# Reciprocal square roots in a two-layer hybrid encoder: a GpSimd power and one Newton step instead of a bit trick and three Newton steps

## The chip, the cores and the metric

The kernel runs on one core of a Trainium2 chip. The metric is the device time of one execution in microseconds (us). The core's engines each work through a queue of their own, in the order in which the program was built: PE (TensorE, matrix products; PEld is its weight load), DVE (VectorE), ACT (ScalarE), POOL (GpSimd) and SP (SyncE, which issues the loads). They wait for one another by semaphores. An instruction whose wait is not over holds up everything behind it on the same engine.

## The reference: two layers of FFN, mixer, FFN

The input x is 256 tokens of width 1024, float32. Each of two layers adds a gated feed-forward network, a mixer and a second feed-forward network, each behind a normalisation of its input. After the second layer comes a last normalisation.

```python
def rms_norm(x, g):
    xf = x.astype(jnp.float32)
    y = xf * lax.rsqrt(jnp.mean(xf * xf, axis=-1, keepdims=True) + EPS)
    return (y * g.astype(jnp.float32)).astype(x.dtype)

def l2_norm(x):
    xf = x.astype(jnp.float32)
    return xf * lax.rsqrt(jnp.sum(xf * xf, axis=-1, keepdims=True) + EPS)

for l in range(DEPTH):
    x = x + 0.5 * swiglu(rms_norm(x, ln_ffn1[l]), ffn1_w_in[l], ffn1_w_out[l])
    x = x + hybrid_mixer(rms_norm(x, ln_mix[l]), ...)
    x = x + 0.5 * swiglu(rms_norm(x, ln_ffn2[l]), ffn2_w_in[l], ffn2_w_out[l])
return rms_norm(x, ln_final)
```

The mixer has three branches: a windowed attention (6 heads), a differential attention (4 heads, with rms_norm over each head's output) and a gated delta rule in both directions (6 heads: a short convolution over q, k and v, silu, l2_norm of q and k, a triangular solve and a scan over chunks of 64 tokens, and rms_norm over each head's output times silu of a gate). Their outputs go through one output projection.

## The kernel before: stages, queues and the places that take a reciprocal root

x stays on chip, channels on the 128 partitions, as 8 blocks of 128 x 256. The weights stream in by 512 KB loads that SP issues; up to 8 are in flight or waiting (`wr`).

In an FFN each product of float32 matrices is made of three products of split halves (L259 to L261). ACT rounds each weight block to its high half `wh` (L253), DVE subtracts to get the low half `wl` (L254), PE multiplies. The norm is folded out: PE works on the unnormalised x, and the factor of each token is multiplied into the results (`rb`, L277). So PE starts an FFN before the norm is known, and the norm's small products stand a few blocks later in PE's queue.

In a mixer, `ORDER` is a list of pieces; it is the order in which the pieces are written down. The tile framework's scheduler then builds each engine's queue from the pieces, by its own estimates of when an operand will be ready, so neighbouring pieces interleave. PE's products there write banks of three small pools of PSUM. `pm`, with two banks, serves among others the projections (`pj`), the attention scores (`pss`) and the output projection (`py`): a third product can't begin until the first one's bank has been read out by DVE or ACT.

The pieces that matter here, in order of the program, with the names of the trace:

- `norm_scale` (L193 to L216), for each norm over the width: PE sums the squares of each token (`f_ps`, `m_ps`, `fin_ps`; L200), DVE scales them (`f_v`, L204), `rsqrt` gives the roots of 128 x 2 values (`f_r`, `m_r`, `fin_r`), and PE spreads them over the partitions (`f_pb`, L209). It is called for the four FFNs (f), the two mixers (m) and the end (fin).
- `qk_norm` (`qn` in `ORDER`, L580 to L593), twice in a mixer: ACT squares (`sqt`), DVE sums to `ss` (L586, L587), `rsqrt` on 128 x 12 values, and DVE multiplies q or k by the result (`raw`, L593). After it PE transposes q and k (`pkq`) and multiplies them (`pq`), and DVE inverts the triangular blocks, row by row (`L`, `Vi`, `pp`; L799 and L800). Between them in DVE's queue stand convolution taps (`pad`, L550), read-outs of projections (`pad<-pj`, L537) and gated outputs (`cs`, L571).
- `diff_norm` (`dn`, L763 to L774), once in a mixer: `rsqrt` on 128 x 8 values.
- `out_norm` (`on`, L1004 to L1013), twice in a mixer, one for each half of the tokens: `rsqrt` on 128 x 6 values (`m0on`), beside the first part of the output projection, whose results DVE adds to x (`x<-x,py`, L1031).

That makes 17 calls of `rsqrt` in both layers: 7 on 128 x 2 (4 f, 2 m, 1 fin), 4 on 128 x 12, 2 on 128 x 8 and 4 on 128 x 6.

Before the change `rsqrt` is 11 instructions on DVE: a shift and an integer subtraction that give a first guess (L167, L169), and three Newton steps of three instructions each (L172, L173, L175). In each of them an operand is the result of the one before.

POOL has little to do: 135 instructions, 82.9 us of the span. Its first arithmetic instruction (`sqacc`, L191) has a row "ISA" ahead of it in its queue, which reloads the engine's library of functions.

Of the kernel before, what the change touches and what calls it, by code (L numbers as in the profile page):

```python
# [7 lines left out]
F32 = mybir.dt.float32  # L8
F32R = mybir.dt.float32r
BF16 = mybir.dt.bfloat16  # L10
I32 = mybir.dt.int32
AF = mybir.ActivationFunctionType
ALU = mybir.AluOpType
# [3 lines left out]
P = 128  # L17
# [40 lines left out]
class Kernel:  # L58
    def __init__(self, ctx, tc, ins, out):
        self.tc, self.nc, self.ins, self.out = tc, tc.nc, ins, out  # L60
        nc = self.nc
        ec = ctx.enter_context
        self.cp = ec(tc.tile_pool(name="cp", bufs=1))
        self.wp = ec(tc.tile_pool(name="wp", bufs=4))
        self.rp = ec(tc.tile_pool(name="rp", bufs=NRAW))
        self.xp = ec(tc.tile_pool(name="xp", bufs=1))
        self.sp = ec(tc.tile_pool(name="sp", bufs=2))
        self.pools = {
            t: ec(tc.tile_pool(name=t, bufs=n, space=PSUM)) for t, n in (("pm", 2), ("pd", 4), ("pt", 2))
        }  # L70
        cp = self.cp
        self.x = self.xp.tile([P, KD, S], F32, tag="x", name="x")
        self.col = cp.tile([P, 150], F32, name="col")
        self.cst = None
        self.onec = cp.tile([P, 1], F32, name="onec")
        nc.vector.memset(self.onec, 1.0)
        warm = cp.tile([P, 1], F32, name="warm")
        nc.scalar.activation(warm, self.onec, AF.Copy)

# [83 lines left out]
    def rsqrt(self, v, n, name, out=None):  # L163

        nc, sp = self.nc, self.sp
        ti = sp.tile([P, n], I32, tag=f"rs_i{n}", name=f"{name}_i")
        nc.vector.tensor_scalar(ti, v.bitcast(I32), 1, None, ALU.arith_shift_right)  # L167
        y = sp.tile([P, n], F32, tag=f"rs_y{n}", name=f"{name}_y")
        nc.vector.tensor_scalar(y.bitcast(I32), ti, -1.0, float(0x5F3759DF), ALU.mult, ALU.add)  # L169
        a = sp.tile([P, n], F32, tag=f"rs_a{n}", name=f"{name}_a")  # L170
        for i in range(3):
            nc.vector.scalar_tensor_tensor(a, v, -0.5, y, ALU.mult, ALU.mult)  # L172
            nc.vector.tensor_tensor(a, a, y, ALU.mult)  # L173
            o = y if i < 2 or out is None else out
            nc.vector.scalar_tensor_tensor(o, a, 1.5, y, ALU.add, ALU.mult)  # L175
        return o

    def sq_add(self, k, eng=None, last=False):
# [1057 lines left out]
```

## Time and profile before

| | |
|---|---|
| time, median of 3 runs | 1163.51 us (1162.44 to 1164.4) |
| the profiled execution: time, span | 1162.4 us, 1160.6 us |
| PE busy | 1122.9 us (97%) |
| DVE busy | 735.1 us (63%), 1442 instructions |
| ACT busy | 523.0 us (45%) |
| POOL busy | 82.9 us (7%) |
| mean granted TensorE clock | 0.978 |

The span runs from the first to the last instruction; 1.8 us of the time lie outside it. The busy time of PE is modelled with overlaps, so 97% says that PE seldom stood still, not that it ran at its peak. Layer 0 has its first FFN from 0 to 199 us, its mixer to about 383 us and its second FFN to about 590 us; layer 1 follows 569 us later, stage by stage, and the last norm begins at 1148 us. POOL is the engine with most room, DVE the one on which the removed instructions stand.

### The profile page before, as it was taken

The page shows a single profiled execution, that of the slowest core. Times are in us where ns is not written, and L with a number is a line of the kernel's source. Part 1 is how long each engine was busy: PE and PEld are TensorE (multiplying, and loading weights), DVE is VectorE, ACT ScalarE, POOL GpSimd, SP SyncE. Part 2 cuts the span into 40 slices and gives each one's busy share as a digit, 9 for nine tenths or more (in the row PEclk, how much of TensorE's full clock was granted, in tenths as well). Part 3 has the DMA queues.
Part 4 walks back from the last instruction along what each step waited for, and adds up shares of the span by engine and source line. Part 5 has one row for each costly group of instructions (what it writes and reads, how often), then busy time and mean ns, then how long its engine had stood idle before and what let it go on. Part 6 is the DMA issues. An engine that isn't in the chain of part 4 may idle for free. (4 is left out here: it accounts for less than half of the span.)

```text
span 1160.6 us, 21957 instructions
## 1 busy us (share of the span) xinstructions
PE 1122.9 (97%) x8970; PEld 1025.6 (88%) x8970; DVE 735.1 (63%) x1442; ACT 523.0 (45%) x967; POOL 82.9 (7%) x135
## 2 busy tenths in 40 slices
PE   7999999998899999999999999999989999999996
PEld 7999999776668999999999999988756789999996
DVE  7666654678746566665566666547886476666643
ACT  6545432263572454544444454414437435445431
POOL 0000002101202100000000000011020020000010
PEclk9999999997899999999999999999978999999998
DMA  9655643521114555565555565534210254556521
GB/s 335 213 184 182 206 165 102 163 79 51 54 56 132 189 174 184 184 204 170 173 173 182 182 201 181 160 117 127 78 51 37 75 193 153 184 183 201 182 89 37
DMA packets 49637, 173.64 MB, mean 150 GB/s; under 512 B 5504, under 2 KB 6784, under 8 KB 49536
## 3 DMA queue, kind: packets, MB, share of 16 engines
q1 hardware_dynamic: 49104, 171.64, 45.1%
q8 instruction: 70, 1.15, 0.4%
q10 hardware_dynamic: 432, 0.60, 0.1%
q14 instruction: 31, 0.25, 0.1%
HBM read 171.17 MB, written 1.05 MB: 148 GB/s over the span
## 5 line engine op out<-in xcount | busy, mean ns | idle before, releaser
L254 DVE TENSOR_TENSOR wl<-wr,wh 128x1024 fp32r<-128x1024 f32 x254 | 310.9, 1225 | 181.9 <-ACT wh L253 181.8
L253 ACT ACTIVATE wh<-wr 128x1024 fp32r<-128x1024 f32 x254 | 267.3, 1053 | 256.2 <-issue 146.4
L261 PE MATMUL ps<-xh,wl 128*128 128x256 f32 x1336 | 378.3, 283 | 0.8 <-DVE wl L254 0.8
L259 PE MATMUL ps<-xh,wh 128*128 128x256 f32 x1336 | 379.0, 284 | 0.1
L260 PE MATMUL ps<-xl,wh 128*128 128x256 f32 x1336 | 378.0, 283 | 0.0
L261 PEld LDWEIGHTS ps<-xh,wl 128*128 128x128 f32 x1336 | 256.4, 192 | 1.2 <-DVE wl L254 1.2
L259 PEld LDWEIGHTS ps<-xh,wh 128*128 128x128 f32 x1336 | 256.4, 192 | 1.0 <-issue 0.6
L260 PEld LDWEIGHTS ps<-xl,wh 128*128 128x128 f32 x1336 | 256.4, 192 | 0.0
L259 PE MATMUL ps<-hh,wh 128*128 128x256 f32 x672 | 190.5, 284 | 0.0
L261 PE MATMUL ps<-hh,wl 128*128 128x256 f32 x672 | 188.0, 280 | 0.0
L260 PE MATMUL ps<-hl,wh 128*128 128x256 f32 x672 | 187.5, 279 | 0.0
L428 PE MATMUL pj<-xf,wr 128*128 128x256 f32 x544 | 132.6, 399 | 2.9 <-issue 2.6
L259 PEld LDWEIGHTS ps<-hh,wh 128*128 128x128 f32 x672 | 125.7, 187 | 3.6
L260 PEld LDWEIGHTS ps<-hl,wh 128*128 128x128 f32 x672 | 126.3, 188 | 0.0
L261 PEld LDWEIGHTS ps<-hh,wl 128*128 128x128 f32 x672 | 126.2, 188 | 0.0
L428 PEld LDWEIGHTS pj<-xf,wr 128*128 128x128 f32 x544 | 106.9, 202 | 19.7 <-issue 3.3
L191 POOL TENSOR_TENSOR sqacc<-sqacc,sqt 128x256 f32<-128x256 f32 x41 | 34.6, 843 | 742.0 <-ACT sqt L187 741.9
L282 ACT ACTIVATE hh<-h 128x256 fp32r<-128x256 f32 x88 | 36.1, 415 | 90.3 <-DVE h L280 90.3
L277 DVE TENSOR_TENSOR t<-ps,f_rb 128x256 f32<-128x256 f32 x88 | 36.9, 424 | 37.7 <-PE ps L261 37.4
L1024 PE MATMUL py<-oT,wr 128*128 128x256 f32 x256 | 59.1, 384 | 0.0
L283 DVE TENSOR_TENSOR hl<-h,hh 128x256 fp32r<-128x256 f32 x88 | 36.8, 423 | 30.4 <-ACT hh L282 30.4
L1024 PEld LDWEIGHTS py<-oT,wr 128*128 128x128 f32 x256 | 47.2, 190 | 7.3 <-DVE x L1031 0.3
(321 smaller groups left out, 1135.7 us busy)
## 6 DMA issues: line engine op xcount, KB each, us to landing
wr<-in_ffn SPq DMA_DIRECT2D x258, 512.0 KB, 3.4
wr<-in_mix SPq DMA_DIRECT2D x50, 512.0 KB, 3.4
wr<-in_mix SPq DMA_DIRECT2D x8, 408.0 KB, 3.1
wr<-in_mix SPq DMA_DIRECT2D x8, 384.0 KB, 3.0
x<-in_x SPq DMA_DIRECT2D x4, 256.0 KB, 4.3
ar<-in_ffn SPq DMA_DIRECT2D x8, 128.0 KB, 3.9
cb<-in_constb SPq DMA_DIRECT2D x1, 588.0 KB, 9.8
out_y<-fo SPq DMA_DIRECT2D x2, 256.0 KB, 2.4
```

Of the source, the lines that this page charges most:

```text
L191: (eng or nc.gpsimd).tensor_tensor(self.sq, self.sq, t, ALU.add)
L253: nc.scalar.activation(h, w, AF.Copy)
L254: nc.vector.tensor_tensor(lo, w, h.bitcast(F32), ALU.subtract)
L259: mm(out, lhsT=ah, rhs=bh, start=start, stop=False)
L260: mm(out, lhsT=ah, rhs=bl, start=False, stop=False)
L261: mm(out, lhsT=al, rhs=bh, start=False, stop=stop)
L277: nc.vector.tensor_tensor(t[:rows], gate, rb[:rows], ALU.mult)
L282: nc.scalar.activation(hh[:n, j, :], h[:n], AF.Copy)
L283: nc.vector.tensor_tensor(hl[:n, j, :], h[:n], hh[:n, j, :].bitcast(F32), ALU.subtract)
L428: mm(ps[:, 0:S], lhsT=w[:, k * P : (k + 1) * P], rhs=xf[:, k, :], start=k == 0, stop=k == KD - 1)
L1024: mm(ps[:, 0:S], lhsT=st["o", q // NBLK][:, c], rhs=oT[:, k, :], start=k == ks[0], stop=k == ks[-1])
```

## The change: what it does

`rsqrt` asks POOL for v to the power of -0.5 (`tensor_tensor` with `pow`, the exponent read from a tile `mhalf` of 128 x 12 that is filled once) and takes one Newton step on DVE, three instructions, where there were eleven. Each call now goes from DVE to POOL and back.

```diff
@@ -74,6 +74,8 @@
         self.onec = cp.tile([P, 1], F32, name="onec")
         nc.vector.memset(self.onec, 1.0)
+        self.mhalf = cp.tile([P, 12], F32, name="mhalf")
+        nc.vector.memset(self.mhalf, -0.5)
@@ -163,16 +165,13 @@
     def rsqrt(self, v, n, name, out=None):
         nc, sp = self.nc, self.sp
-        ti = sp.tile([P, n], I32, tag=f"rs_i{n}", name=f"{name}_i")
-        nc.vector.tensor_scalar(ti, v.bitcast(I32), 1, None, ALU.arith_shift_right)
         y = sp.tile([P, n], F32, tag=f"rs_y{n}", name=f"{name}_y")
-        nc.vector.tensor_scalar(y.bitcast(I32), ti, -1.0, float(0x5F3759DF), ALU.mult, ALU.add)
+        nc.gpsimd.tensor_tensor(y, v, self.mhalf[:, 0:n], ALU.pow)
         a = sp.tile([P, n], F32, tag=f"rs_a{n}", name=f"{name}_a")
-        for i in range(3):
-            nc.vector.scalar_tensor_tensor(a, v, -0.5, y, ALU.mult, ALU.mult)
-            nc.vector.tensor_tensor(a, a, y, ALU.mult)
-            o = y if i < 2 or out is None else out
-            nc.vector.scalar_tensor_tensor(o, a, 1.5, y, ALU.add, ALU.mult)
+        nc.vector.scalar_tensor_tensor(a, v, -0.5, y, ALU.mult, ALU.mult)
+        nc.vector.tensor_tensor(a, a, y, ALU.mult)
+        o = y if out is None else out
+        nc.vector.scalar_tensor_tensor(o, a, 1.5, y, ALU.add, ALU.mult)
         return o
```

The change is ahead of most of the program, so the lines from `sq_add` on have a number that is 1 smaller than before. The scheduler also builds other queues from it. Two places on DVE show what that means.

The first is DVE's queue at the first `qk_norm` of layer 0 (`ss` holds the sums of squares, `m0qk` names the root's tiles, `cs` is a gated convolution output, `pad` a convolution's input, `pj` a projection). Before:

```order
L587 TENSOR_SCALAR ss_2745<-ss_2745 128x12 [waits DVE_49]
L167 TENSOR_SCALAR m0qk_i<-ss_2745 128x12 [waits DVE_49]
L571 SCALAR_TENSOR_TENSOR cs<-th,pad 128x128 [waits PE_49,Activation_49]
L169 TENSOR_SCALAR m0qk_y<-m0qk_i 128x12 [waits DVE_49]
L571 SCALAR_TENSOR_TENSOR cs<-th,pad 128x128
L172 SCALAR_TENSOR_TENSOR m0qk_a<-ss_2745,m0qk_y 128x12 [waits DVE_49]
L537 TENSOR_TENSOR pad<-pj,m_rb 128x2x64 [waits PE_49]
L173 TENSOR_TENSOR m0qk_a<-m0qk_a,m0qk_y 128x12 [waits DVE_49]
L537 TENSOR_TENSOR pad<-pj,m_rb 128x128
L175 SCALAR_TENSOR_TENSOR m0qk_y<-m0qk_a,m0qk_y 128x12 [waits DVE_49]
```

And with the change:

```order
L586 TENSOR_SCALAR ss_2731<-ss_2731 128x12 [waits DVE_49]
L171 SCALAR_TENSOR_TENSOR m0qk_a<-ss_2731,m0qk_y 128x12 [waits Pool_49]
L570 SCALAR_TENSOR_TENSOR cs<-th,pad 128x128 [waits PE_49,Activation_49]
L172 TENSOR_TENSOR m0qk_a<-m0qk_a,m0qk_y 128x12 [waits DVE_49]
L570 SCALAR_TENSOR_TENSOR cs<-th,pad 128x128
L174 SCALAR_TENSOR_TENSOR m0qk_y<-m0qk_a,m0qk_y 128x12 [waits DVE_49]
L536 TENSOR_TENSOR pad<-pj,m_rb 128x2x64 [waits PE_49]
L592 TENSOR_TENSOR raw_2700<-raw_2700,m0qk_y 128x384 [waits DVE_49]
L592 TENSOR_TENSOR raw_2700<-raw_2700,m0qk_y 128x384
L536 TENSOR_TENSOR pad<-pj,m_rb 128x128
L549 SCALAR_TENSOR_TENSOR pad<-pad,cwh 128x256 [waits Activation_49]
```

The instruction that waits for POOL stands directly behind the sums, with nothing between; and the second half of the read-out of a projection (L536, before L537), which stood ahead of the multiplication of `raw`, and the convolution taps that need it, now stand behind that multiplication.

The second is DVE's queue at the two `out_norm` pieces of layer 0 (`hvo` holds a norm's sums, `po` and `pw` are products of the scan, `x<-x,py` reads out the output projection, `wl` is a weight half of the next FFN). From the first norm's sums to the second's root it now reads:

```order
L1008 TENSOR_SCALAR hvo<-hvo 128x6 [waits DVE_49]
L171 SCALAR_TENSOR_TENSOR m0on_a<-hvo,m0on_y 128x6 [waits Pool_49]
L172 TENSOR_TENSOR m0on_a<-m0on_a,m0on_y 128x6 [waits DVE_49]
L174 SCALAR_TENSOR_TENSOR m0on_y<-m0on_a,m0on_y 128x6 [waits DVE_49]
L1011 TENSOR_SCALAR m0on_y<-m0on_y,rth 128x6 [waits DVE_49]
L1012 TENSOR_TENSOR O<-zt,m0on_y 128x384 [waits DVE_49]
L993 TENSOR_TENSOR SC<-po,egc 128x384 [waits PE_49]
L995 TENSOR_TENSOR O<-O,SC 128x384 [waits DVE_49]
L1030 TENSOR_TENSOR x<-x,py 128x256 [waits PE_49]
L1001 TENSOR_TENSOR O<-O,pw 128x384 [waits DVE_49,PE_49]
L1009 TENSOR_TENSOR zt<-zt,O 128x384 [waits DVE_49]
L1007 TENSOR_REDUCE hvo<-on 128x6 [waits Activation_49]
```

and goes on from there:

```order
L1008 TENSOR_SCALAR hvo<-hvo 128x6 [waits DVE_49]
L171 SCALAR_TENSOR_TENSOR m0on_a<-hvo,m0on_y 128x6 [waits Pool_49]
L253 TENSOR_TENSOR wl<-wr,wh 128x1024 [waits DMAHW0_49,Activation_49]
L172 TENSOR_TENSOR m0on_a<-m0on_a,m0on_y 128x6 [waits DVE_49]
L1030 TENSOR_TENSOR x<-x,py 128x256 [waits PE_49]
L174 SCALAR_TENSOR_TENSOR m0on_y<-m0on_a,m0on_y 128x6 [waits DVE_49]
```

Before, the second of these two read-outs stood ahead of the second norm's first root instruction, and the weight half stood ahead of that norm's sums:

```order
L1008 TENSOR_REDUCE hvo<-on 128x6 [waits Activation_49]
L254 TENSOR_TENSOR wl<-wr,wh 128x1024 [waits DMAHW0_49,Activation_49]
L1009 TENSOR_SCALAR hvo<-hvo 128x6 [waits DVE_49]
L1031 TENSOR_TENSOR x<-x,py 128x256 [waits PE_49]
L167 TENSOR_SCALAR m0on_i<-hvo 128x6 [waits DVE_49]
L169 TENSOR_SCALAR m0on_y<-m0on_i 128x6 [waits DVE_49]
```

Now both the weight half and that read-out stand behind the instruction that waits for POOL.

On PE the order differs at the norms: between the sums `f_ps` and the spread roots `f_pb` of an FFN stood 27 products (47 in the first FFN), and now 8 (18 in the first); between `m_ps` and `m_pb` four products are now two. In the mixer's middle some transposes and projections trade places, and from the first `pT` of the attention on, PE's order is the same in both. On POOL each power stands in the queue between the instructions that were there, and the row "ISA" now stands ahead of the first power of the first FFN.

## The prediction

> **What bounds the kernel now.** I read the page's busy table first, then the windows of the first mixer, the waits of PE, and the timeline at the places that call `rsqrt`.
>
> ```profile
> PE 1122.9 (97%) x8970; PEld 1025.6 (88%) x8970; DVE 735.1 (63%) x1442; ACT 523.0 (45%) x967; POOL 82.9 (7%) x135
> 40.00:60.00 20.00, 20.00 (x169) 20.00 (x169) 13.52 (x20) 9.66 (x15) 0.00 (x0) 1.00 0.64 211
> 280.00:300.00 20.00, 19.00 (x69) 13.02 (x68) 17.80 (x26) 8.04 (x27) 4.40 (x4) 0.80 0.17 54
> 300.00:320.00 20.00, 15.99 (x73) 12.88 (x72) 13.52 (x25) 11.28 (x34) 4.34 (x2) 0.83 0.08 26
> 360.00:380.00 20.00, 20.00 (x168) 17.02 (x164) 16.02 (x47) 7.25 (x11) 3.31 (x10) 1.00 0.54 178
> PE pss L675 <- ACT sc L719: 6.6, 2, 4.0
> PE fin_pb L209 <- DVE fin_r L175: 2.4, 1, 2.4
> ```
>
> A window's columns are its length, then the busy time of PE, PEld, DVE, ACT and POOL, the granted TensorE clock and the DMA share. In the FFNs (40 to 60) PE is full, so a norm there costs only what PE waits for it. The mixer is full on PE again from 320 on. Between, PE has holes and DVE is busiest (17.80 of 20). The largest hole of each mixer, 4.0 us here and 2.6 in layer 1, ends a chain that starts at `qk_norm`:
>
> ```profile
> 249.53 1.02 DVE L593 TENSOR_TENSOR raw<-raw,m0qk_y 128x384 f32<-128x384 f32 x2
> 250.22 0.85 PE L412 MATMUL pkq<-cst,raw 128*128 128x128 f32 x6 [0.91 <-DVE raw L593]
> 303.10 1.22 DVE L800 TENSOR_REDUCE Vi<-pr 128x64 f32<-128x1024 f32 x1 [4.00 <-POOL pr L799]
> 306.09 2.07 PE L675 MATMUL pss<-wq 64*128 64x256 f32 x4 [4.01 <-ACT sc L719]
> 818.95 0.85 PE L412 MATMUL pkq<-cst,raw 128*128 128x128 f32 x6 [0.91 <-DVE raw L593]
> 874.77 1.88 PE L675 MATMUL pss<-wq 64*128 64x256 f32 x4 [2.55 <-ACT sc L719]
> ```
>
> From the transposes behind the second `qk_norm` to that product it takes 55.87 us in layer 0 and 55.82 in layer 1, though PE's holes differ. So what delays the second `raw` delays the mixer's end by as much.
>
> **The price of a power.** No power is in the trace. Its bounds come from POOL's other rows:
>
> ```profile
> L191 POOL TENSOR_TENSOR sqacc<-sqacc,sqt 128x256 f32<-128x256 f32 x41 | 34.6, 843 | 742.0 <-ACT sqt L187 741.9
> L799 POOL TENSOR_TENSOR pr<-L,Vi 128x8 f32<-128x8 f32 x2 | 0.4, 212 | 32.7 <-DVE Vi L800 32.7
> 226.89 0.17 DVE L491 COPY gc<-pg 128x24 f32<-128x24 f32 x1
> 227.13 0.22 POOL L499 CAST g<-gc 128x24 bf16<-128x24 f32 x1 [2.87 <-DVE gc L491]
> 213.50 1.67 DVE L474 SCALAR_TENSOR_TENSOR sr<-sr,z 128x48 f32<-128x48 f32 x7
> ```
>
> At the cheap end it is one more elementwise operation: 0.2 us at any of our sizes. One pass over an element costs (843 - 212)/(256 - 8) = 2.5 ns. [...] This kernel writes a logarithm out by itself, on DVE: the seven steps of its series (L474, 14 operations) and nine operations around them, 23 in all. As many again for the exponential and some fifteen for exponent, product and special cases make 60, that is 150 ns an element: 0.5 us for 2, 1.1 for 6, 1.4 for 8, 2.0 for 12. I take this estimate, since a power is nearer to that code than to an addition; for the dear end I allow 80 operations: 0.6, 1.4, 1.8 and 2.6 us. The ways there and back are short: `gc` ends at 227.06 and POOL starts on it at 227.13, 0.07 us; I allow 0.05 back.
>
> The Trainium skill, "GPSIMD Engine Reference", section 7, has a rule against the change: a chain of dependent float32 operations costs 4 cycles an element for each, at 1.2 GHz. By it 60 operations would be an estimated 2.6 us for 12 elements, and the time would be that of the dear end; no run here shows it yet.
>
> **The end.** The last norm hides behind nothing:
>
> ```profile
> 1150.53 0.16 DVE L204 TENSOR_SCALAR fin_v<-fin_ps 128x2 f32<-128x2 f32 x1 [1.43 <-PE fin_ps L200]
> 1152.70 0.16 DVE L175 SCALAR_TENSOR_TENSOR fin_r<-fin_a,fin_y 128x2 f32<-128x2 f32 x1
> ```
>
> From the one start to the other lie eleven steps of (1152.70 - 1150.53)/11 = 0.197 us, so the root ends 2.17 us after `fin_v` does. Now it is 0.07 + 0.5 + 0.05 + 2 x 0.197 + 0.16 = 1.17: a gain of **1.0 us** (1.3 to 0.9).
>
> **The FFNs.** PE now meets the spread roots 19 products earlier.
>
> ```profile
> 401.82 0.16 DVE L204 TENSOR_SCALAR f_v<-f_ps 128x2 f32<-128x2 f32 x1 [1.02 <-PE f_ps L200]
> 405.01 0.16 DVE L175 SCALAR_TENSOR_TENSOR f_r<-f_a,f_y 128x2 f32<-128x2 f32 x1
>   DVE f_r L175: 0.9, 3
> 1140.53 0.28 PE L259 MATMUL ps<-hh,wh 128*128 128x256 f32 x1
> 1140.65 0.28 PE L260 MATMUL ps<-hl,wh 128*128 128x256 f32 x1
> ```
>
> PE waits 0.9 us for `f_r` in three of the four, 0.3 each, so in this one it arrives at 404.9. Products start 0.118 apart; 19 fewer bring it there at 402.66. The root is ready 1.17 us after `f_v` ends (401.98), at 403.15: a wait of 0.5 in place of 0.3. With the same for the first FFN, whose DVE queue holds a weight half between the steps, I take a loss of **0.9 us** for all four (0 to 1.3).
>
> **The mixer's q and k.** Before, eleven short instructions were dealt out among long ones that filled their latency:
>
> ```profile
> 235.61 0.17 DVE L587 TENSOR_SCALAR ss<-ss 128x12 f32<-128x12 f32 x1
> 237.89 0.49 DVE L550 SCALAR_TENSOR_TENSOR pad<-pad,cwh 128x256 f32<-128x256 f32 x1 [0.16 <-ACT pad L544]
> 239.85 1.02 DVE L593 TENSOR_TENSOR raw<-raw,m0qk_y 128x384 f32<-128x384 f32 x2
> 243.33 0.95 DVE L586 TENSOR_REDUCE ss<-sqt 128x12 f32<-128x768 f32 x1 [1.66 <-ACT sqt L584]
> ```
>
> Now DVE stands at the first root from 235.8 to 237.9 (0.07 + 2.0 + 0.05), and the gated outputs, the read-out, the taps and all else wait behind. `raw` then comes at 238.7, 1.1 earlier, but the second half of the read-out is behind it, so ACT's first tap (0.5) ends at 240.55 and DVE's taps start at 240.6, where they started at 237.89: 2.7 later. Through the gated output, transposes and squares of the other of q and k this reaches the second sum at 246.3 instead of 243.33: some 0.3 us more. It ends at 247.85, the root waits until 250.0, six short and half-hidden instructions follow, and the second `raw` stands at 251.2 instead of 249.53: **1.7 us later** in each mixer. Each tenth of a microsecond in the power counts here about twice: 1.7 + 2 x 0.6 = 2.9 at the dear end and 1.7 - 2 x 1.8 = -1.9 at the cheap one. Against it goes m's root, which is 1.0 us earlier as at the end; DVE waits for PE's projections and for ACT behind it, so I count 0.4. Both mixers: **+2.6 us** (-4.6 to +5.0).
>
> **The two output norms.** Here a queue behind DVE's wait meets PE where it is full:
>
> ```profile
> 362.07 0.16 DVE L1009 TENSOR_SCALAR hvo<-hvo 128x6 f32<-128x6 f32 x1
> 364.70 0.41 DVE L1031 TENSOR_TENSOR x<-x,py 128x256 f32<-128x256 f32 x1
> 365.31 11.06 PE L1024 MATMUL py<-oT,wr 128*128 128x256 f32 x50
> 367.69 1.23 DVE L254 TENSOR_TENSOR wl<-wr,wh 128x1024 fp32r<-128x1024 f32 x1 [0.17 <-ACT wh L253]
> 368.90 0.41 DVE L1031 TENSOR_TENSOR x<-x,py 128x256 f32<-128x256 f32 x1
> 376.20 0.82 PE L412 MATMUL pto<-cst,O 128*128 128x128 f32 x6
> ```
>
> The 50 products are five output blocks of ten, 0.221 us each, on two banks. The third block starts at 365.31 + 20 x 0.221 = 369.73 and needs the bank of the first, which DVE reads out from 368.90 to 369.31: 0.4 us of slack. Now: the first root's wait ends at 363.45, three steps and the two instructions behind (L1011, L1012) at 364.8; the scan's three and the first read-out at 366.65, the second sum at 368.15; POOL until 369.3; then the first step, the weight half (1.2) and the second step, and only then the read-out, 370.7 to 371.1. PE stands for **1.4 us** in each mixer, 2.9 in both (none at the cheap end, 4.1 at the dear). The second norm's own result has cover: transposes want it at 376.2, five microseconds after the late read-out.
>
> `dn` costs nothing. Its eleven steps, 2.2 us, become a wait of 1.5 and three steps, 2.1, and the copies behind it wait for ACT anyway:
>
> ```profile
> 340.53 0.56 DVE L915 COPY W<-p 32x384 f32<-32x384 f32 x1 [2.40 <-ACT W L915]
> ```
>
> Were that cover gone, it would still gain 0.1 us (0.4 us lost at the dear end). The reload of POOL's library moves ahead of the first power; POOL is idle from 1 us to that power at 22.
>
> **The sum.** -1.0 + 0.9 + 2.6 + 2.9 = +5.4 us on the profiled execution's 1162.4: 1167.8. That execution was the fastest of the three shown, 1.1 under their median, so I write it on the median: 1168.9, rounded to **1169**. The ends sum to -5.9 and +9.5.
>
> **Rivals.** (1) *The power is cheap.* At 0.2 us all waits vanish, and the mixers gain what the second `raw` gains: 1163.5 - 5.9 = 1157.6. For it: the 212 ns row. Against: that row is one multiplication. It decides below about 80 ns an element, 1.1 us for 12, where the sum crosses zero.
>
> (2) *The power is dear*, 80 operations: 1163.5 + 9.5 = 1173.0. This is also where the rule of the Trainium skill's "GPSIMD Engine Reference" on dependent chains leads. Nothing in the trace tells 60 from 80.
>
> (3) *The delay of q and k is absorbed.* In the inversion DVE waits for PE's scores:
>
> ```profile
> 282.74 0.69 DVE L716 TENSOR_REDUCE mxd<-pss 128x2 f32<-128x512 f32 x1 [1.12 <-PE pss L713]
> ```
>
> Maxima that move behind a row of the inversion could take such waits up. Then +2.6 falls to about -0.8 and the sum to +2.0: 1165.5. Against: both layers keep 55.8 us.
>
> (4) *The clock halves once more.* After holes the granted clock drops:
>
> ```profile
> 304.00:305.00 1.00, 0.00 (x0) 0.00 (x0) 1.00 (x3) 0.00 (x0) 0.00 (x0) 0.99 0.00 0
> 305.00:306.00 1.00, 0.00 (x0) 0.00 (x0) 1.00 (x1) 0.98 (x5) 0.00 (x0) 0.50 0.00 0
> 312.00:313.00 1.00, 1.00 (x6) 0.90 (x5) 0.64 (x2) 0.99 (x2) 0.00 (x0) 1.00 0.00 0
> ```
>
> Some 6.6 us at half clock cost 3.3 of work. If PE, waiting for the transposes of the gated outputs that now stand behind the first root, drops there in both layers and can't make it up, the time is 1168.9 + 6.6 = 1175.5. For it: this drop came 2.9 us into the hole of 4.01 us that ends at 306.09, and the new wait is about 2 us. Against: PE has holes behind it to catch up. The Trainium skill, "TensorE: Matmul & The Clock Gate", part 1, asks for an idle window of about 3.4 us; the row's 2.9 us is a little under it, and the measurement decides.
>
> **How the numbers follow.** The forecast has 0.50, rivals 1 to 4 have 0.13, 0.12, 0.15 and 0.10. A change under 0.2% (2.3 us) can't be told from none: rival 3 is the same, rival 1 faster, the forecast and the other two slower: 0.13, 0.15, 0.72. From 1162 to 1175 leaves out most of rival 1 and the upper half of rival 4. The slower cases alone span 1166 to 1175.
>
> **What would show it.** On POOL, powers of 0.5, 1.1 and 2.0 us by size, or 0.2 for all. On DVE, idle time before the first root step, ended by POOL, some 17 times and about 21 us in all (7 x 0.62, 4 x 2.12, 2 x 1.52 and 4 x 1.22 give 20.7). Among PE's waits, a new one of 1.4 us for a read-out ahead of `py`, twice; `pkq` 1.7 us later against the mixer's start. I am wrong if `pkq` isn't late, or if PE's output projection runs on without a hole.

## The result: 1179.1 us, 15 us slower than before, and the profile after

| | before | after |
|---|---|---|
| time, median of 4 runs | 1163.87 us (1162.44 to 1164.4) | 1179.06 us (1178.13 to 1180.26) |
| ratio, 95% interval | | 1.0133 (1.0116 to 1.0151) |
| the profiled execution: time, span | 1162.4, 1160.6 us | 1178.51, 1176.7 us |

The direction was forecast, the size was not: 1169 was the forecast and 1175 the upper end of the range. The busy table and four windows of the kernel after:

```profile
PE 1128.8 (96%) x8970; PEld 1030.3 (88%) x8970; DVE 716.7 (61%) x1307; ACT 523.9 (45%) x967; POOL 103.3 (9%) x152
240.00:260.00 20.00, 17.34 (x95) 13.40 (x93) 11.92 (x35) 13.29 (x44) 3.21 (x2) 0.94 0.25 80
280.00:300.00 20.00, 19.67 (x57) 12.63 (x57) 16.78 (x25) 8.60 (x29) 2.54 (x2) 0.66 0.09 27
300.00:320.00 20.00, 15.58 (x63) 11.54 (x62) 14.39 (x23) 9.49 (x30) 6.17 (x3) 0.83 0.08 27
360.00:380.00 20.00, 18.30 (x246) 15.09 (x243) 13.72 (x32) 4.49 (x8) 4.66 (x12) 1.00 0.25 83
```

Two things stand out. PE's window from 360 on, full before, now has a hole of 1.7 us. And PE is busy for 5.9 us more (1128.8 against 1122.9) with the same 8970 products, which no step of the prediction has.

The power itself, in POOL's groups (count, then busy time and mean ns of one), and the waits of DVE that it ends (total, times, longest):

```profile
L169 POOL TENSOR_TENSOR m0qk_y<-ss,mhalf 128x12 f32<-128x12 f32 x2 | 4.5, 2275 | 13.3 <-DVE ss L586 13.3
L169 POOL TENSOR_TENSOR m0dn_y<-hv,mhalf 128x8 f32<-128x8 f32 x1 | 1.6, 1648 | 25.0 <-DVE hv L768 25.0
L169 POOL TENSOR_TENSOR m0on_y<-hvo,mhalf 128x6 f32<-128x6 f32 x2 | 2.7, 1327 | 7.4 <-DVE hvo L1008 7.4
L169 POOL TENSOR_TENSOR f_y<-f_v,mhalf 128x2 f32<-128x2 f32 x4 | 2.8, 706 | 50.7 <-DVE f_v L203 50.7
```

```profile
DVE m1qk_a L171 <- POOL m1qk_y L169: 4.6, 2, 2.4
DVE f_a L171 <- POOL f_y L169: 3.3, 4, 0.8
DVE m1on_a L171 <- POOL m1on_y L169: 2.9, 2, 1.4
DVE fin_a L171 <- POOL fin_y L169: 0.8, 1, 0.8
```

A power costs (2275 - 706)/10 = 157 ns an element and 0.39 us besides. All 17 waits together take 24.3 us of DVE, where some 21 were forecast.

PE's waits after:

```profile
PE ptr L411 <- DVE cs L570: 5.5, 2, 2.8
PE pss L707 <- DVE dqk L661: 5.4, 2, 2.7
PE pkq L411 <- ACT tap L546: 4.5, 2, 2.3
PE py L1023 <- DVE x L1030: 3.3, 2, 1.7
PE f_pb L208 <- DVE f_r L174: 2.1, 4, 0.6
PE fin_pb L208 <- DVE fin_r L174: 1.6, 1, 1.6
```

`py` is the hole that was forecast. `ptr`, 2.8 us in each layer, is not in the forecast's sum: PE stands ahead of a transpose, in both mixers, behind the first root of q and k (rival 4 reckoned with such a wait, of about 2 us). (`pkq` is put down to ACT's tap, which came last by the profile; what it needs is `raw`, which DVE writes from 253.91 on, below.)

**The first of the two roots for q and k**, on DVE and then on PE (start, duration, idle time before in brackets):

```profile
238.88 0.17 DVE L171 SCALAR_TENSOR_TENSOR m0qk_a<-ss,m0qk_y 128x12 f32<-128x12 f32 x1 [2.39 <-POOL m0qk_y L169]
239.53 0.29 DVE L536 TENSOR_TENSOR pad<-pj,m_rb 128x128 f32<-128x128 f32 x1
240.67 0.29 DVE L536 TENSOR_TENSOR pad<-pj,m_rb 128x128 f32<-128x128 f32 x1
242.16 2.05 DVE L549 SCALAR_TENSOR_TENSOR pad<-pad,cwh 128x256 f32<-128x256 f32 x4 [1.20 <-ACT pad L543]
245.65 0.29 DVE L536 TENSOR_TENSOR pad<-pj,m_rb 128x128 f32<-128x128 f32 x1 [1.44 <-PE pj L427]
248.84 0.95 DVE L585 TENSOR_REDUCE ss<-sqt 128x12 f32<-128x768 f32 x1
252.65 0.17 DVE L171 SCALAR_TENSOR_TENSOR m0qk_a<-ss,m0qk_y 128x12 f32<-128x12 f32 x1 [2.19 <-POOL m0qk_y L169]
253.91 1.02 DVE L592 TENSOR_TENSOR raw<-raw,m0qk_y 128x384 f32<-128x384 f32 x2
```

```profile
239.31 0.47 PE L411 MATMUL ptr<-cst,cs 128*128 128x128 f32 x1 [2.77 <-DVE cs L570]
240.61 2.06 PE L427 MATMUL pj<-xf,wr 128*128 128x256 f32 x4
242.85 3.62 PE L427 MATMUL pj<-xf,wr 128*128 128x256 f32 x16
817.74 0.33 PE L411 MATMUL ptr<-cst,cs 128*128 128x128 f32 x1 [2.76 <-DVE cs L570]
818.44 1.11 PE L427 MATMUL pj<-xf,wr 128*128 128x256 f32 x4
```

The read-outs of the projection are split: one half at 239.53, the other behind `raw` at 240.67, as forecast. But the gated outputs `cs` also stood behind the first wait. PE's transposes of them are ahead of the projections in its queue, so the projections too came after the power, and at 245.65 DVE waits for PE. The same four products take 2.06 us in layer 0 and 1.11 in layer 1. The granted clock says why (windows of 1 us, the clock is the third number from the end):

```profile
241.00:242.00 1.00, 1.00 (x3) 0.76 (x3) 0.00 (x0) 1.00 (x6) 0.00 (x0) 0.50 0.00 0
818.50:819.50 1.00, 1.00 (x10) 0.85 (x7) 0.89 (x3) 1.00 (x7) 0.00 (x0) 1.00 0.06 16
```

**The second output norm**, on DVE and on PE:

```profile
374.00 0.17 DVE L1008 TENSOR_SCALAR hvo<-hvo 128x6 f32<-128x6 f32 x1
375.61 0.17 DVE L171 SCALAR_TENSOR_TENSOR m0on_a<-hvo,m0on_y 128x6 f32<-128x6 f32 x1 [1.43 <-POOL m0on_y L169]
375.69 1.23 DVE L253 TENSOR_TENSOR wl<-wr,wh 128x1024 fp32r<-128x1024 f32 x1
```

```profile
377.37 6.74 PE L1023 MATMUL py<-oT,wr 128*128 128x256 f32 x30 [1.67 <-DVE x L1030]
```

This is the forecast picture: first step, weight half, and PE waiting for the read-out behind them.

**The end and the FFNs.** The last root ends 1.53 us after `fin_v` begins (2.33 before):

```profile
1167.42 0.16 DVE L203 TENSOR_SCALAR fin_v<-fin_ps 128x2 f32<-128x2 f32 x1 [1.43 <-PE fin_ps L199]
1168.79 0.16 DVE L174 SCALAR_TENSOR_TENSOR fin_r<-fin_a,fin_y 128x2 f32<-128x2 f32 x1
```

The products of the FFNs' second half, before and then after, in PE's groups:

```profile
L260 PE MATMUL ps<-hl,wh 128*128 128x256 f32 x672 | 187.5, 279 | 0.0
```

```profile
L259 PE MATMUL ps<-hl,wh 128*128 128x256 f32 x672 | 190.1, 283 | 0.0
```

They wait for nothing in either, and yet each is 4 ns longer. Counted by their starts, the 2016 products of the second halves are 0.1178 us apart before and 0.1199 after. Those of the first halves are 0.1200 apart in both. The 2.1 ns that each product of the second halves loses make 4.2 us.

Stage by stage, by the starts of the same instructions in both profiled executions (span +16.1): the four FFNs +1.2 and three times +1.5, the mixers +6.0 and +4.8, the end -0.8, the start +0.3.

### The profile page after: what moved, and what is told of

It reads as the page before. It is cut to its first block, busy times and chain, and to the rows that moved or that the text cites. A ratio compares the mean times of both kernels' runs of the same rounds, so it can differ in the third digit from the quotient of the medians.

```text
span 1176.7 us, 21818 instructions
## 1 busy us (share of the span) xinstructions
PE 1128.8 (96%) x8970; PEld 1030.3 (88%) x8970; DVE 716.7 (61%) x1307; ACT 523.9 (45%) x967; POOL 103.3 (9%) x152
## 5 line engine op out<-in xcount | busy, mean ns | idle before, releaser
L258 PE MATMUL ps<-hh,wh 128*128 128x256 f32 x672 | 193.0, 287 | 0.0
L259 PE MATMUL ps<-hl,wh 128*128 128x256 f32 x672 | 190.1, 283 | 0.0
L258 PEld LDWEIGHTS ps<-hh,wh 128*128 128x128 f32 x672 | 128.7, 191 | 3.5
L259 PEld LDWEIGHTS ps<-hl,wh 128*128 128x128 f32 x672 | 128.8, 192 | 0.0
L260 PEld LDWEIGHTS ps<-hh,wl 128*128 128x128 f32 x672 | 128.8, 192 | 0.0
```

The lines of the kernel that those rows point to most:

```text
L258: mm(out, lhsT=ah, rhs=bh, start=start, stop=False)
L259: mm(out, lhsT=ah, rhs=bl, start=False, stop=False)
L260: mm(out, lhsT=al, rhs=bh, start=False, stop=stop)
```

## Experiments

Two questions: where do the slower products come from, and why did q and k cost so much more than forecast?

### Places and queues apart

The change adds a tile of 48 bytes ahead of all others and takes the integer tiles away, so weights move up by 64 bytes and the hidden values down by 256. Address modulo 256 in SBUF: the weights stand at 224, the FFN's input at 224 and the hidden values at 32 before; all three at 32 after. The first kernel has the old instructions (and one fill more) at the new addresses:

```diff
+        self.mhalf = cp.tile([P, 12], F32, name="mhalf")
+        nc.vector.memset(self.mhalf, -0.5)
...
-        ti = sp.tile([P, n], I32, tag=f"rs_i{n}", name=f"{name}_i")
+        a = sp.tile([P, n], F32, tag=f"rs_a{n}", name=f"{name}_a")
+        ti = a.bitcast(I32)
```

> The kernel before, instruction for instruction, but every tile stands at the SBUF address that it has in the kernel after (a column of 48 bytes more in front, the integer tiles of the roots gone). Theory A, that the place of the tiles made the products of the FFNs' second half start 0.120 us apart in place of 0.1177: PE busy 1128.8 in place of 1122.9, and the time is the kernel before plus 5 to 7 us. Theory B, that the products were slowed by the changed engines beside them (POOL's powers, DVE's waits): no change, within 1 us of the kernel before, spacing 0.1177.

The second has the new queues at the old addresses: the exponents lie in the padding of `onec`, and `y` takes the room of the integer tiles.

```diff
+        one = cp.tile([P, 16], F32, name="onec")
+        self.onec, self.mhalf, warm = one[:, 0:1], one[:, 1:13], one[:, 13:14]
...
-        y = sp.tile([P, n], F32, tag=f"rs_y{n}", name=f"{name}_y")
+        y = sp.tile([P, -(-n // 8) * 16], F32, tag=f"rs_y{n}", name=f"{name}_y")[:, 0:n]
```

> The change complete, in the same order on every engine, but the tiles stand where they stood in the kernel before. Theory A (place): 5 to 7 us under the kernel after, 1172 to 1174, products of the FFNs' second half 0.1177 apart, and what is left over the kernel before (about 9 us) is the price of the waits. Theory B (engines): 1179 like the kernel after, spacing 0.120.

Measured: old instructions at new places 1167.34 us against 1163.69, ratio 1.0036 (1.0023 to 1.0049). New queues at old places 1175.73, ratio 1.0102 (1.0089 to 1.0116). The group rows, places moved first, places put back second:

```profile
L262 PE MATMUL ps<-hl,wh 128*128 128x256 f32 x672 | 190.1, 283 | 0.0
```

```profile
L267 PE MATMUL ps<-hl,wh 128*128 128x256 f32 x672 | 187.5, 279 | 0.0
```

The slow products follow the places and not the queues. Theory A holds, theory B falls: 3.3 to 3.7 us of the 15.2 are placement, and 12.0 are left for the waits. Its sizes were off: 5 to 7 us were expected of the places and about 9 of the waits.

### The price of the operation, with the queues unchanged

```diff
-        nc.vector.memset(self.mhalf, -0.5)
+        nc.vector.memset(self.mhalf, 1e-3)
...
-            nc.gpsimd.tensor_tensor(y, v, self.mhalf[:, 0:n], ALU.pow)
+            nc.gpsimd.tensor_tensor(y, v, self.mhalf[:, 0:n], ALU.mult)
```

> As the one before, same order and same places, but the power is a multiplication by 0.001 on the same engine, so the roots and all that follows from them are wrong; only the price of the operation differs. If the price of the power makes the loss (the forecast's term for q and k and the output norms, and its first rival), the waits fall from 0.7 / 1.3 / 2.3 us to about 0.3 and the time to 1156 to 1160. If it is the new order of the queues (projections behind the gated outputs on PE, the read-out behind the root on DVE), it stays over the kernel before by 2 us or more: 1166 to 1170.

Measured: 1158.46 us, ratio 0.996 (0.9947 to 0.9972). The price was the cause, and the first rival's 1157.6 was a good number for it. Powers take 22.5 us in all, the multiplications 3.4; between them lie 19.1 us, and the kernel is 17.3 shorter. The part of `dn` is covered (2.9 us; from `hv` to the first `pto` nothing changes), so 16.2 at most are the price itself; the half clock shown above, which is gone too, adds to it.

Where it goes shows a table of the stages around q and k (us, from the starts of the rows of DVE and PE; layer 0 / layer 1). A "sum" is the row `ss<-ss` behind the reduction. The kernels of its last two columns come further below.

| stage | before | new queues, old places | multiplication | first root a multiplication | q and k alone |
|---|---|---|---|---|---|
| `m_v` to first sum of q, k | 27.67 / 27.01 | 26.86 / 26.85 | 26.44 / 26.43 | 26.85 / 26.85 | 27.66 / 27.00 |
| first to second sum | 8.71 / 8.72 | 13.89 / 12.36 | 10.29 / 10.29 | 10.28 / 10.29 | 12.35 / 13.75 |
| second sum to second `raw` | 5.21 / 5.20 | 3.81 / 3.81 | 1.75 / 1.75 | 3.82 / 3.81 | 3.81 / 3.80 |
| first sum to second `raw` (the two rows above) | 13.92 / 13.92 | 17.70 / 16.16 | 12.04 / 12.04 | 14.10 / 14.10 | 16.16 / 17.55 |
| second `raw` to the `pss<-wq` behind the longest wait (2.6 to 4.1 us) | 56.56 / 56.52 | 56.60 / 57.88 | 57.80 / 57.57 | 57.83 / 58.12 | 58.35 / 57.96 |

In the second row the new queue with a multiplication costs 1.6 us (10.29 against 8.71), the dear power 2.07 more, which is all of its price, and one layer of each execution loses another 1.4 to 1.5. The third row gives some back. Together they bring the second `raw` 2.2 us later than before, or 3.6 to 3.8 where those 1.4 to 1.5 come on top, and 1.9 earlier with the multiplication. The last row grows by 1.0 to 1.8 us in seven of eight layers, with the power or without. In the kernels further below that keep the old queue here (the power for the output norms alone, or for the norms of the residual stream alone) it takes 56.3 to 56.5 as before.

### One part of the change at a time

The condition is the size: 12, 6 or 2 values; all other roots stay as before, and so do the places.

```diff
+        power = n == 12
```

> The power and one step for q and k alone (12 values), the other roots as before, all tiles at the places of the kernel before. The prediction's step (second product of the roots 1.7 us later in each mixer): 1163.7 + 3.4 = 1167. The trace of the kernel with the change and the old places (second sum 5 us later against the first in each layer, of which the shorter root gives 1.4 back): 3.3 to 3.6 each, 1170 to 1171.

> The power and one step for the two output norms alone (6 values). The prediction's step (PE stands 1.4 us for a read-out that is queued behind the second root): 1163.7 + 2.9 = 1166.6. By the trace of the changed kernel (1.7 us each, and the transposes behind 1.95 later): 1167.4. If the hole is paid back by what follows: within 1 us of 1163.7.

> The power and one step for the norms of the residual stream alone (2 values: four FFNs, two mixers, the last). The prediction's steps: -1.0 at the end, +0.9 in the FFNs, -0.8 for the mixers: 1162.8. By the traces since: -0.8 at the end, +0.5 in each of three or four FFNs, -0.5 for the mixers: 1163.5 to 1164.2. The three kernels with one part each should add up to the +12 of the complete change at the old places.

| the power for | time, us | ratio, 95% | forecast of the step |
|---|---|---|---|
| q and k | 1173.43 | 1.0085 (1.0071 to 1.0099) | +3.4 |
| output norms | 1166.06 | 1.0027 (1.0016 to 1.0037) | +2.9 |
| FFNs, mixers, end | 1162.70 | 0.9996 (0.9987 to 1.0005) | -0.9 |

Against 1162.85 before, q and k cost 10.6 us, the output norms 3.2, and the norms of the residual stream nothing that can be told. The sum of the ratios' excesses, 0.0108, agrees with the 0.0102 of the complete change at the old places, so the parts add up. Two steps of the forecast were right and one was too small by 7 us. The 1170 to 1171 that were worked out for q and k from the trace were too low as well. In the profiled execution of that kernel, 1171.31 us, the later second `raw` and the longer last row of the table make 9.1 us; its other executions took 1172.64 to 1174.28, and what they add was not traced.

### What stands behind the first wait

First the order: the first root's steps are queued on DVE behind the gated outputs, with the power for q and k alone.

```diff
-E:1 qn:1 co:0:0 co:0:1
+E:1 qn:1 co:0:0 co:0:1 qm:1
...
+            def qk_scale(a):
+                raw = st["raw", a]
+                with ExitStack() as behind:
+                    if a == 1:
+                        behind.enter_context(tc.issue_after(st["cs"].ins))
+                    rq = st["rq", a]().rearrange("p (t h) -> p t h", t=2)
```

> As the kernel with the power for q and k alone, but the first root's first step is queued on DVE behind the two gated outputs that stood behind its wait, so PE's transposes and the projections behind them don't wait for the power. Theory C, that the loss at q and k comes from what is queued behind the first wait: the second sum falls back to its old distance from the first (8.7 us in place of 13.9), PE's wait of 2.8 us ahead of the transposes is gone, and the time is 1162 to 1166. Theory D, that the price of the power lies on the path by itself (root of one of q and k after the other): within 1.5 us of the kernel with the power for q and k alone.

Measured: 1177.93 us, ratio 1.0128 (1.0114 to 1.0141), slower still. Both numbers were missed. The place did what theory C says, in part: the sums are 11.38 and 11.37 us apart, not 8.7, but 1.0 and 2.4 less than in the same layers without the edit, and the second `raw` comes 1.1 later than before in both layers, where the kernel without the edit has 2.2 and 3.6. But the scheduler dealt out the rest of the mixer anew. PE's waits in this kernel:

```profile
PE pkq L424 <- DVE raw L612: 7.8, 4, 2.2
PE pss L727 <- DVE wq L678: 7.0, 2, 3.7
PE ptr L424 <- DVE cs L583: 2.7, 6, 1.2
```

`ptr` is down from 7.2 us to 2.7. The waits for `wq`, 7.0 us in place of 0.7, stand where PE waited 8.0 us for `sc` without the edit, and that wait is down to 0.9. What was won is given back behind `raw`: from the second `raw` to `hv` of `dn` the mixers take 2.9 and 4.1 us more than without the edit. As a test of the whole it decides nothing, since it changes more than it means to.

Then the price, with the queues unchanged: only the first root of each mixer is a multiplication.

```diff
+            first = "qk1" in name
+            w = self.small[:, 0:1].to_broadcast([P, n]) if first else self.mhalf[:, 0:n]
+            nc.gpsimd.tensor_tensor(y, v, w, ALU.mult if first else ALU.pow)
```

> The complete change at the old places, same order, but the first of the two roots for q and k in each mixer is a multiplication by 0.001 (so k is scaled wrongly and what follows from it is wrong); all other powers stay. Theory E, that every microsecond of the power lies on the path through DVE's queue: 2 x 2.07 off 1175.7, so 1171.6. Theory F, that PE's hole of 2.8 us behind the first wait also costs clock (1.4 us once in an execution): 1170.2, and no slice at half clock behind it. If the first root's price is hidden and only the second's counts: 1175.

Measured: 1169.36 us, ratio 1.0053 (1.0041 to 1.0065), 6.4 under the complete change at the old places. PE's wait is 0.7:

```profile
PE ptr L423 <- DVE cs L582: 1.4, 2, 0.7
```

No slice behind it is at half clock, and the sums are 10.28 and 10.29 us apart. By the times alone theory E can't be told from F, since the gain is 5.7 us by the ratios, with 2.1 either way. The traces decide for F: the layer without the half clock gains 2.07 us between the sums, which is the first root's price in full, and the layer with it 3.6.

That the hole sets the clock off was not tried apart from the price. Four of the profiled executions have the hole of 2.76 or 2.77 us, and in each of them one of the two layers had 3.41 us at half clock behind it; where there was no such hole, none had. The clock records say why it was one layer and not both. In every profiled execution here the granted clock changes only at marks 3.41 us apart (239.18 and 242.59 in the kernel after). The hole, cut at these marks:

| kernel | layer | most of the hole between two marks, us | half clock from the second mark on |
|---|---|---|---|
| after | 0 / 1 | 2.63 / 1.71 | yes / no |
| new queues, old places | 0 / 1 | 2.24 / 1.71 | yes / no |
| q and k alone | 0 / 1 | 1.93 / 2.55 | no / yes |
| complete change at 192 (below) | 0 / 1 | 2.70 / 1.38 | yes / no |

So in these eight holes it depended on how the hole fell between the marks. This is no limit for other places: elsewhere in the mixers the clock fell behind stretches in which PE stood still for less.

### The distance of a product's operands

A gap of 64 bytes ahead of the residual stream moves the FFN's input and all behind it, and no instruction.

```diff
+        self.xp.tile([P, 16], F32, tag="gap", name="gap")
         self.x = self.xp.tile([P, KD, S], F32, tag="x", name="x")
```

> The kernel before with a gap of 64 bytes ahead of the residual stream, so that the normed input of each FFN (and all behind it) stands 64 bytes further from the weights; no instruction differs. Theory A, in the form that products are slow where the streamed operand and the weights have the same address modulo 256 (as the input and the weights have in both kernels, the hidden values only in the kernel after): the 4000 products of the FFNs' first half fall from 0.120 to 0.1177 us, the second half stays at 0.1177, and the time falls by 8 to 10 us to 1154. Theory B: no change.

Measured: 1151.99 us (1148.78 to 1155.3), ratio 0.9911 (0.9896 to 0.9927), 11.7 us where 8 to 10 were expected: two of the first halves were faster than 0.1177, and the second halves, which moved too, slower (table below). The next gap is twice as wide, and the one after keeps the hidden values where they were.

> The kernel before with a gap of 128 bytes ahead of the residual stream: input and weights of the first half 128 apart modulo 256, hidden values and weights of the second half 192 apart. If the distance modulo 256 alone counts: the first half as the second half did at 128 (a product's mean 281 to 286 ns in place of 283 to 284 at 0 and 278 at 64; little gain), the second half as at 64 if distances work both ways; 1157 to 1162. If any distance but 0 is as good as 64: 1144 to 1148.

> The kernel before, instruction for instruction, with both halves' operands 64 bytes from the weights modulo 256 (64 bytes ahead of the residual stream, the hidden values where they were). The kernel with the gap alone was 11.7 us faster although its second half lost about 1.6 us in each of three groups of products; without that loss 16 us faster: 1147.

> The places of the one before, and the power with one step for the two mixers' first norms and for the last norm alone, the norms whose roots came earlier in the trace (0.45 us each and 0.8). 1.7 us under the one before: 1145.5. If those gains are absorbed by later waits: no difference.

Measured: 1151.51 (1150.87 to 1152.08), ratio 0.9896 (0.9883 to 0.9909); 1153.59 (1142.33 to 1155.03), ratio 0.9886 (0.9854 to 0.9918); and, with the power for three norms besides, 1151.84 (1148.83 to 1156.07), ratio 0.9898 (0.9881 to 0.9916). The 1147 of the third lies at the edge of its interval, the fourth missed its 1145.5, and 1.7 us between these two can't be told from this spread. With 1151.5 the second lies between the numbers of both forms of the rule. Its second halves were the fastest so far, so 192 was given to both halves:

> The kernel before, instruction for instruction, with both halves' streamed operands 192 bytes above the weights modulo 256. If the distance modulo 256 sets how far apart products start (0.120 us at 0, 0.1178 at 64 with some FFNs at 0.114, 0.1187 to 0.120 at 128, 0.1137 at 192, all from second halves or first halves so far, 192 from second halves alone): the 4000 products of the first half gain 25 us, the 2000 of the second 8: 1130. If 192 helps the second half alone: 1153 to 1156.

> The complete change with the same places as the one before. If place and waits are two separate causes, the change costs the 10 to 13 us here that it costs at the old places: 1140 to 1143. If the faster products take up the waits or meet them sooner, less than 8 or more than 15.

> The places of these two, and the power with one step for the two mixers' first norms and the last norm alone: 1.7 us under the first of the three (0.45 twice and 0.8) if those gains survive, no difference if later waits absorb them.

Measured: 1135.2 us (1128.77 to 1146.83), ratio 0.9736 (0.9713 to 0.9758); with the complete change 1145.41 (1144.52 to 1150.52), ratio 0.9857 (0.9838 to 0.9875); with the power for three norms 1132.55 (1128.87 to 1138.6), ratio 0.974 (0.9717 to 0.9763). The first two were expected at 1130 and at 1140 to 1143. Group rows of the last, input and hidden values:

```profile
L268 PE MATMUL ps<-xl,wh 128*128 128x256 f32 x1336 | 370.6, 277 | 0.0
L268 PE MATMUL ps<-hl,wh 128*128 128x256 f32 x672 | 185.8, 277 | 0.0
```

Mean distance of starts in us, by FFN, in the profiled executions:

| streamed operand minus weights, modulo 256 | first halves | second halves |
|---|---|---|
| 0 | 0.1200 in all | 0.1199 (after) |
| 64 | 0.1178, 0.1178, 0.1137, 0.1138 (gap of 64); 0.1175 to 0.1178 in all (both kernels with 64 for both halves) | 0.1178 (before) |
| 128 | 0.1188, 0.1199, 0.1199, 0.1187 | 0.1187 |
| 192 | 0.1136, 0.1178, 0.1135, 0.1135 (the last kernel); 0.1174 to 0.1178 in all (old instructions) | 0.1136 to 0.1142 |

So the distance matters. At 0 every FFN had the slow pace, with the weights at 224 and at 32; and the hidden values, at 32 in both kernels of this study, went from 0.1178 to 0.1199 when the weights moved. The other distances were tried with the weights at 224 alone. The mixers' projections gained nothing (132.6 us of PE before, 132.4 to 134.5 with the gaps). And the distance isn't all: at 64 and 192 a first half has one of two paces, though all four FFNs of a kernel have their operands at the same addresses. What picks between them stays open. It fits the spread of these times: the faster pace is worth 4.1 us in each first half, the profiled execution of 1146.83 us at 192 had it in none of the four, and that of the last kernel, 1132.81 us, in three.

Place and waits add up within this spread: the change costs 10.2 us by the medians here, 14 by the ratios, 12.0 at the old places. Both kernels at 192 without the large powers beat the two kernels of this study by some 30 and 45 us; whether the three small powers help is not to be told.

## Why the prediction was wrong

**The price was nearly right.** Estimated at 150 ns an element and 0.2 us, measured 157 and 0.39. That is 0.2 to 0.3 us a call more than the terms had. The dear end's 200 ns an element was not reached. That end was also where the Trainium skill's "GPSIMD Engine Reference", section 7, led with the 60 operations that I assumed; the trace is under it, and what the library really computes no run shows. No run shows the 60 operations either, on which 0.5, 1.1, 1.4 and 2.0 us rest; the runs show 0.71, 1.33, 1.65 and 2.28.

**The end and the FFNs.** -1.0 came out as -0.8, the power being 0.2 dearer. In the FFNs PE waits 2.1 us for `f_r` in place of 0.9, +1.2 where +0.9 was forecast; by the intervals at the old places the FFNs lose 1.6. The parts offset each other with the mixers' first norms (0.8 and 0.2 earlier), which is why that kernel alone shows nothing.

**The output norms.** Right: 1.67 us of hole where 1.4 stood, with each power 0.2 dearer; 3.2 us for both mixers alone, +2.9 forecast. **`dn`** is as free as forecast: from `hv` to the first `pto` 9.26 us in both kernels and layers.

**The step that failed** is the last one on q and k: "So what delays the second `raw` delays the mixer's end by as much." It put the change of the stretch behind `raw` at nothing, because both layers of the kernel before take the same time for it. That the two layers agree says nothing of another queue, and the queue there is another. The stretch is 1.0 to 1.8 us longer in seven of eight layers, also with a multiplication in the power's place, and keeps its length where the old queue stands. So the new queue does that and not the wait. In it the first attention read-out stands behind two more taps (before, then after; `raw` begins at 249.53 and 253.91), and the first maximum comes 1.6 us later against `raw`:

```profile
250.86 0.42 DVE L662 SCALAR_TENSOR_TENSOR dqk<-pj,m_rb 128x256 f32<-128x256 f32 x1
275.51 0.68 DVE L716 TENSOR_REDUCE mxd<-pss 128x2 f32<-128x512 f32 x1
```

```profile
257.07 0.42 DVE L661 SCALAR_TENSOR_TENSOR dqk<-pj,m_rb 128x256 f32<-128x256 f32 x1
281.45 0.68 DVE L715 TENSOR_REDUCE mxd<-pss 128x2 f32<-128x512 f32 x1
```

That this row makes the difference is likely, but it was not tried alone.

**The chain up to the second `raw`** was right but for the price. "Through the gated output, transposes and squares of the other of q and k this reaches the second sum at 246.3 instead of 243.33": 3.0 us later; the same row is 3.4 later, or 4.8 to 4.9 where the clock halves. The second `raw` is 2.2 us later where the clock holds, forecast 1.7. The power is 0.27 us dearer and counts twice, as the prediction says, which makes 1.7 + 2 x 0.27 = 2.24. At the cheap end it has -1.9, and the multiplication gave -1.88. What it left out of the sum is PE: the transposes of `cs` stand ahead of the projections there, and behind the hole of 2.8 us the clock fell in one of the layers.

**Rival 4 was half right.** The clock does halve once more, at the place that the rival named, but in one layer of two, for 3.41 us, and at a cost of 1.4 to 1.5 us, not 3.3 in each. (The drop from which the rival took its 3.3 lasted 6.8 us, not 6.6.) The Trainium skill, "TensorE: Matmul & The Clock Gate", part 1 ("What's actually happening"), tells of a window of about 3.4 us that runs freely, so that the same work falls into it differently. The traces agree: the marks 3.41 us apart, and equal holes of 2.76 and 2.77 us, four with a drop and four without, by how they fell between the marks. That an idle time under the page's window was enough, they show too: 2.24 us between two marks were followed by a drop.

**The term that was missing** is the placement, 3.3 to 3.7 us. No row of the prediction speaks of addresses. The hint was in the trace: products of one shape ran 0.120 us apart in one half of an FFN and 0.1178 in the other. The prediction even used the second number and did not ask why it wasn't the first.

**The miss in one sum.** Measured are 15.2 us, forecast were 5.4. Of the 9.8 between them some 3.5 are placement, 1.5 the clock, 1.4 the stretch behind `raw` (as the profiled execution at the old places has it), 1.1 the dearer power at q and k, and 1.3 the same at the end, in the FFNs and at the output norms. About 1 us is not accounted for.

## What to carry to other kernels

An operation that goes to another engine and back can cost its whole duration on the engine that waits, and again on every queue that this engine feeds, as at q and k, or nothing, as at `dn`: follow the wait through each queue. Where a change also gives a queue another order, the stretch behind it has to be read again row by row; its old length proves nothing. A change that adds or drops even a small tile moves everything allocated behind it; before a difference of some tenths of a per cent is put down to the instructions, the old instructions should be timed at the new addresses. And where two groups of equal products run at different paces, their operands' addresses are worth a look: here 2.6% lay in setting the streamed operands 192 bytes from the weights, modulo 256.

## What the runs showed of the hardware that was not expected

- The pace of PE's products (128 x 128 weights, 128 x 256 streamed, split float32) depends on where the two operands lie to each other in SBUF, modulo 256 bytes: 0.1200 us at 0, 0.1136 at best at 192. The Trainium skill, "TensorE: Matmul & The Clock Gate", part 2 ("Step-by-step: what each phase is for"), has two independent read ports, by which the next weights' load takes nothing from a running product. The measured pace differs with the place at the same instructions; what in the chip makes it so, and why a first half at 64 or 192 has one of two paces at the same addresses, stays open.
- A power on GpSimd costs 0.71 us for 2 columns and 2.28 for 12, a multiplication 0.20 and 0.21. The reload of its library, ahead of the first power, was hidden in POOL's idle time: its row stands at 1.0 us, and the first power, at 22.2, waited for DVE.
- The granted clock changed only at marks 3.41 us apart. Of eight equal holes of 2.8 us, the four of which 2.24 to 2.70 us lay between two marks were followed by 3.41 us at 0.50, the four with 1.38 to 1.93 by none.
